# One more seven-product quad in three passes of a hybrid attention and state-space block

## The chip, the cores and the metric

The kernel runs on one core of a Trainium2 chip. The metric is device time in microseconds of one execution; before the change it is 1381.21 us, the median of three runs (1380.38 to 1382.6). Five engines work side by side, each through its own instructions in a fixed order, and wait for each other by semaphores: TensorE (PE, matrix products), VectorE (DVE), ScalarE (ACT), GpSimd (POOL) and SyncE (SP), whose queue issues nearly all DMA transfers.

## The reference

One layer on 256 rows of 2048 features, all in fp32:

```python
hn = rms_norm(x, norm_w)
q, k, v, z_a, z_s, xbc, dt_raw, g_a, g_s = split(hn @ w_in)
o_a = dilated_attention(q, k, v) * silu(z_a)            # 16 heads, three patterns
y = rms_norm(ssd_scan(conv(xbc), dt_raw) * silu(z_s))   # 4096 wide
merged = sigmoid(g_a) * (o_a @ w_attn_branch) + sigmoid(g_s) * (y @ w_ssm_branch)
out = rms_norm(x + merged @ w_out, final_norm_w)
```

Nearly all of the work is in the products with the weights: `w_in` is 2048 by some 22,600, `w_attn_branch` and `w_out` are 2048 by 2048, `w_ssm_branch` 4096 by 2048.

## The kernel before

**Precision by halves.** A weight unit is 128 x 1024 fp32 values (512 KB), fetched by SP into a ring of five buffers (tag `w`). ACT copies it into a rounded high half `h` (L279), DVE subtracts that for the low half `l` (L280), and PE makes each product from three matmuls, high by high, high by low and low by high (L485 to L487 in `triple`). The activations were split the same way.

**Passes and quads.** The second half of the kernel is mostly passes through `gemm_pair`, each making 1024 output columns of all 256 rows: the state-space branch, then v (two passes, named by their first block of 512 columns: v0, v2), the gate passes ga0 and ga2, the attention branch attn0 and attn2, and out0 and out2. Between v and ga the 16 heads' q, k and z_a are projected and the attention is done. From v on a pass sums over 16 row blocks of the weights, taken in eight quads of two: two row blocks, two halves of the rows, two blocks of 512 columns. A plain quad uses two units as they come and 24 matmuls of 512 columns. A seven-product quad is a step of Strassen's scheme in Winograd's form: seven products in place of eight, 21 matmuls. Its weights need more work. SP fetches the first unit (`wa`), half of the second (`wc`) and a combination of both made earlier (`wt`, under the name of the tile that holds it: th_a in the gate passes, fin in the attention branch). ACT and DVE split them into four pairs: ha, la from wa; hc, lc from wc; htt, ltt from wt; and, after DVE has subtracted half of wt from wa in place (L566), htu, ltu from wa (L552, L553). A number behind such a name is the unit it comes from: ga0 begins at unit 385, ga2 at 401, attn0 at 417, attn2 at 433; quad q of a pass starts at its first unit + 2q.

**Buffers that set the order.** The t and u pairs come from a pool with two buffer pairs (tags `ht`, `lt`, `bufs=2`); only the v passes have two more. The other pairs come from a pool of four. A seven-product quad adds some products directly into the outputs' accumulators (`es`, ps_ in the trace) and others into four accumulators of its own kind (`prods`, pp_), which are combined at the end of the pass by `fold` (two copies on ACT, L590 and L591, and four DVE operations, L592 to L595) and then added to the outputs (L1022 in the gate passes, L1159 in the attention branch). In the attention branch each block is then merged with the gates (L1148, L1149), and the merged rows are turned by PE transposes (`turn_m`, tiles mtp) for the output product.

**Sums made ahead.** `sum_jobs` makes the combinations wt behind certain weight units of an earlier stage, with two DVE operations each, and stores them in DRAM; those for ga, attn and out are made while the heads are projected. Likewise the activations' combinations (`sx`) are stored and fetched back by `fetch_left`: a one-element copy on GpSimd behind a named unit (L441), then a transfer on SP's queue (L442).

**What sets the order.** Each engine's order is fixed when the program is built: a scheduler walks the program with modelled times, and conversions run ahead of their use by a priority (`L_AHEAD`). The table `S_QUADS` says which quads of each pass have seven products, `G_ORDERS`, `A_ORDERS` and `V_ORDERS` in which order a pass takes its quads. PE's order interleaves a plain quad with the seven-product quads beside it.

Of the kernel before, what the change touches and what calls it, by code (L numbers as in the profile page):

```python
# [23 lines left out]
KT = D // P  # L24
UNIT = 1024
# [14 lines left out]
GS_BEFORE = {0: (0, 1), 4: (2,)}  # L40
A_ORDERS = {0: (0, 1, 2, 4, 3, 6, 5, 7), 2: (0, 2, 1, 4, 3, 5, 6, 7)}
V_ORDERS = {0: (0, 2, 4, 1, 3, 5, 6, 7), 2: (0, 2, 1, 4, 3, 5, 6, 7)}
G_ORDERS = {c: (0, 2, 1, 4, 3, 5, 6, 7) for c in (0, 2)}
O_LEFT = {0: {0: (0, 3), 4: (1, 5)}, 2: {}}
# [155 lines left out]
def hybrid_block(ctx: ExitStack, tc: tile.TileContext, wall, xt, x, pk_d, cst_d, fw_d, out):  # L200
# [34 lines left out]
    def behind_unit(n, f):  # L235
        on_unit.setdefault(n, []).append(f)
# [457 lines left out]
    with tc.tile_pool(name="ssm", bufs=2) as sp:  # L694
# [332 lines left out]
    xl = ctx.enter_context(tc.tile_pool(name="xl", bufs=1))  # L1027
    dc = xl.tile([P, 768], F32, name="dc", tag="dc")
    dist_c, count_c = dc[:, :384], dc[:, 384:]
    behind_unit(FIRST[("v", 2)] + 1, lambda behind: fetch(dc, cst_d[:, :768], behind))  # L1030
    room = room_of(big.tile([P, 6 * 512], F32, name="room_v", tag="yo0a"), 2, 2)
    with tc.tile_pool(name="vx", bufs=1) as vx:
        tl = big.tile([P, 4, UNIT], F32R, name="tl_v", tag="yo0b")
        room["tl"] = [(tl[:, 2 * n], tl[:, 2 * n + 1]) for n in range(2)]
        for n, q in enumerate(SX_V):
            fetch_left(sx_of_x, vx, len(SX_V), ("x", q), two_kts(XT, q), 0, FIRST[("v", 0)])
        for n, q in enumerate(SX_X[1:]):
            fetch_left(sx_of_x, xl, len(SX_X) - 1, ("x", q), two_kts(XT, q), 0, FIRST[("v", 0)] + 1 + n)
        for c in (0, 2):
            es, prods = gemm_pair(  # L1040
                ("v", c), lambda kt: XT[:, kt, :], KT, sx_of_x, c == 2, order=V_ORDERS[c], room=room
            )
            dst = blocks(vt, c)
            fold(prods, dst)
            for d, e in zip(dst, es):
                ve.tensor_tensor(d, e, d, ALU.add)
    sx_of_o = {}

    with tc.tile_pool(name="att", bufs=2) as ap:
# [4 lines left out]
        def scores(h, q, k, p):  # L1054
# [28 lines left out]
        def mix(h, pT, za):  # L1083
# [204 lines left out]
```

## Time and profile before

| | before |
|---|---|
| median of three runs | 1381.21 us |
| profiled execution | 1381.23 us |
| its span, first to last instruction | 1379.5 us |
| PE busy | 1368.6 us, 99% |
| DVE busy | 1169.1 us, 85% |
| ACT busy | 835.2 us, 61% |
| POOL busy | 153.5 us, 11% |
| DMA, mean | 250 GB/s |

The span is read from one profiled execution; 1.73 us of its time lie outside it. The shares are means over stages of different kinds, so the stages are read one by one, in windows and timelines. PE's matmuls are pipelined: a record is longer than the distance to the next, and the distance from start to start is what a matmul takes of the span. The same holds for rows of DVE and ACT that follow each other without a gap.

### The profile page before, as it was taken

To read this page: it belongs to the slowest core of one execution; us is meant where nothing else is said; L and a number is where in the kernel's file an instruction comes from. 1 tells how busy PE (TensorE), PEld (TensorE's weight loads), DVE (VectorE), ACT (ScalarE), POOL (GpSimd) and SP (SyncE) were. 2 spreads that over 40 slices of the span, in tenths; PEclk is the share of its full clock that TensorE was granted. 3 is DMA by queue.
4 is the path that set the end of the run, shared out by engine and by line. 5 is a ranking of instruction groups with operands and counts; after the bars stand their busy time and mean duration, and the time that the engine had idled before them with its cause. 6 is when DMAs were issued, how large, how long until landed. Compare 5 with 4: busy or idle time off the path is not lost.

```text
span 1379.5 us, 20706 instructions
## 1 busy us (share of the span) xinstructions
PE 1368.6 (99%) x7266; PEld 1167.4 (85%) x7266; DVE 1169.1 (85%) x1753; ACT 835.2 (61%) x1306; POOL 153.5 (11%) x226
## 2 busy tenths in 40 slices
PE   9999999999999999999999999999999999999997
PEld 7888888888888888888888888888888888888886
DVE  6898899888899898779989887777877788888897
ACT  7655776675667676666565554454445556655564
POOL 2301221101011100010001001211111000000122
PEclk9999999999999999999999999999999999999999
DMA  9767878778787867568677668888888757865783
GB/s 342 231 192 234 294 271 288 260 238 294 251 276 234 304 202 221 174 232 286 229 259 273 208 220 281 281 277 275 289 287 296 243 165 268 291 222 176 244 274 122
DMA packets 105080, 345.00 MB, mean 250 GB/s; under 512 B 11728, under 2 KB 13712, under 8 KB 104976
## 3 DMA queue, kind: packets, MB, share of 16 engines
q1 hardware_dynamic: 103536, 339.62, 73.7%
q10 hardware_dynamic: 1440, 4.06, 0.8%
q8 instruction: 57, 0.93, 0.3%
q14 instruction: 47, 0.39, 0.1%
HBM read 314.87 MB, written 28.77 MB: 249 GB/s over the span
## 4 chain that ended last, share of the span: by engine, by line
PE 98%; DMA 0%; DVE 0%; ACT 0%; issue 0%; SPq 0%; POOL 0%; POOLq 0%; DVEq 0%
PE ps_xs L334 8%; PE ps_zs L334 8%; PE ps_k L334 4%; PE ps_za L334 4%; PE ps_q L334 4%; PE ps_zs L340 4%; PE ps_xs L340 4%; PE ps_ssm L486 3%; PE ps_ssm L487 3%; PE ps_ssm L485 3%; PE ps_q L340 2%; PE ps_za L340 2%; PE ps_k L340 2%; PE ps_gs L423 2%; PE ps_gs L422 2%; PE ps_gs L421 2%
## 5 line engine op out<-in xcount | busy, mean ns | idle before, releaser
L279 ACT ACTIVATE h<-w 128x1024 fp32r<-128x1024 f32 (+1 forms) x398 | 413.5, 1048 | 308.2 <-issue 80.2
L280 DVE TENSOR_TENSOR l<-w,h 128x1024 fp32r<-128x1024 f32 (+1 forms) x398 | 478.5, 1209 | 116.5 <-ACT h L279 112.1
L334 PE MATMUL ps_zs<-XT,h 128*128 128x512 f32 x496 | 172.0, 393 | 0.0
L334 PE MATMUL ps_xs<-XT,h 128*128 128x512 f32 x496 | 171.6, 394 | 0.0
L340 PE MATMUL ps_zs<-XT,l 128*128 128x256 f32 x496 | 134.6, 279 | 0.0
L340 PE MATMUL ps_xs<-XT,l 128*128 128x256 f32 x496 | 133.7, 278 | 0.0
L334 PEld LDWEIGHTS ps_xs<-XT,h 128*128 128x128 f32 x496 | 91.4, 188 | 19.4
L334 PEld LDWEIGHTS ps_zs<-XT,h 128*128 128x128 f32 x496 | 91.3, 188 | 18.9
L340 PEld LDWEIGHTS ps_zs<-XT,l 128*128 128x128 f32 x496 | 93.4, 188 | 2.1
L340 PEld LDWEIGHTS ps_xs<-XT,l 128*128 128x128 f32 x496 | 93.2, 188 | 2.1
L334 PE MATMUL ps_q<-XT,h 128*128 128x512 f32 x256 | 91.1, 404 | 0.0
L334 PE MATMUL ps_k<-XT,h 128*128 128x512 f32 x256 | 88.6, 395 | 0.0
L334 PE MATMUL ps_za<-XT,h 128*128 128x512 f32 x256 | 88.4, 394 | 0.0
L552 ACT ACTIVATE ha<-wa 128x1024 fp32r<-128x1024 f32 x43 | 45.4, 1055 | 44.7 <-PE ps_ssm L487 10.2
L340 PE MATMUL ps_q<-XT,l 128*128 128x256 f32 x256 | 68.5, 278 | 0.0
L340 PE MATMUL ps_k<-XT,l 128*128 128x256 f32 x256 | 68.4, 278 | 0.0
L340 PE MATMUL ps_za<-XT,l 128*128 128x256 f32 x256 | 68.4, 277 | 0.0
L553 DVE TENSOR_TENSOR la<-wa,ha 128x1024 fp32r<-128x1024 f32 x43 | 52.4, 1218 | 10.1 <-ACT ha L552 9.3
L553 DVE TENSOR_TENSOR ltu<-wa,htu 128x1024 fp32r<-128x1024 f32 x38 | 46.3, 1219 | 15.3 <-ACT htu L552 15.2
L795 ACT ACTIVATE gt<-acb,acT 128x128 f32<-128x128 f32 x128 | 44.1, 390 | 23.7 <-DMA acb<-acum_d 23.7
L334 PEld LDWEIGHTS ps_k<-XT,h 128*128 128x128 f32 x256 | 47.0, 188 | 9.8
L334 PEld LDWEIGHTS ps_q<-XT,h 128*128 128x128 f32 x256 | 47.1, 188 | 9.6
(688 smaller groups left out, 3328.0 us busy)
## 6 DMA issues: line engine op xcount, KB each, us to landing
w<-in_wall SPq DMA_DIRECT2D x394, 512.0 KB, 4.8
wa<-in_wall SPq DMA_DIRECT2D x43, 512.0 KB, 4.8
th_a<-in_wall SPq DMA_DIRECT2D x19, 512.0 KB, 5.5
sums_at<-in_wall SPq DMA_DIRECT2D x18, 512.0 KB, 5.0
acb<-acum_d SPq DMA_DIRECT2D x32, 256.0 KB, 3.7
t_ssm<-sums_at SPq DMA_DIRECT2D x13, 512.0 KB, 4.6
wt<-t_ssm SPq DMA_DIRECT2D x13, 512.0 KB, 4.9
th_a<-in_wall SPq DMA_DIRECT2D x19, 256.0 KB, 5.9
```

The lines of the kernel that those rows point to most:

```text
L279: ac.activation(h[:, a:b], w[:, a:b], AF.Copy)
L280: ve.tensor_tensor(l[:, a:b], w[:, a:b], h[:, a:b].bitcast(F32), ALU.subtract)
L334: high = pe.matmul(acc, h[:, kk, :], xs_of(kt), start=(kt == 0), stop=False)
L340: low = pe.matmul(acc[:, S:], l[:, kk, :], xs_of(kt)[:, :S], start=False, stop=(kt == KT - 1))
L421: pe.matmul(accs[i], xh, h[:, kk], start=(kt == 0), stop=False)
L422: pe.matmul(accs[i], xh, l[:, kk], start=False, stop=False)
L485: pe.matmul(acc, xh, h, start=start, stop=False)
L486: pe.matmul(acc, xh, l, start=False, stop=False)
L487: pe.matmul(acc, xl, h, start=False, stop=stop)
L552: ac.activation(h, src, AF.Copy)
L553: ve.tensor_tensor(l, src, h.bitcast(F32), ALU.subtract)
L795: ac.activation(g4[:, n, b], acb[:, j, b // 2 * P : b // 2 * P + P], AF.Relu, scale=-1.0, bias=sc[:, h : h + 1],)
```

## The change

In both gate passes quad 3 becomes a seven-product quad, and the quads are taken in the order 0, 2, 4, 1, 3, 5, 6, 7, as in v0: the plain quad 1 parts 2 and 4 from the run 3, 5, 6. In attn0 quad 5 becomes one, and the order is 0, 1, 2, 4, 5, 6, 3, 7: two plain quads, four seven-product quads, two plain ones. Three more sums are made ahead (22 for 19), one every 3.75 units from the fourth unit of the heads on, where it was every fourth from the eighth. The activations' combination of quad 3, which had a pool of its own in the v passes, joins the others in the pool that lasts through the gate passes. The tile `dc` with the heads' distances and counts goes: these are now fetched into the mask's place and two other pieces, by three small transfers. Three small tiles of `rsqrt_rows` become one. The fetches of the activations' combinations for the attention branch (sx_o) go from SP's queue to GpSimd's, and the first of them is tied to unit 404 where it was 408. The lines behind L40 move up by one to five: L279 becomes L278, L552 L551, L592 L591, L1148 L1143, L1159 L1154.

```diff
-A_ORDERS = {0: (0, 1, 2, 4, 3, 6, 5, 7), 2: (0, 2, 1, 4, 3, 5, 6, 7)}
+A_ORDERS = {0: (0, 1, 2, 4, 5, 6, 3, 7), 2: (0, 2, 1, 4, 3, 5, 6, 7)}
 V_ORDERS = {0: (0, 2, 4, 1, 3, 5, 6, 7), 2: (0, 2, 1, 4, 3, 5, 6, 7)}
-G_ORDERS = {c: (0, 2, 1, 4, 3, 5, 6, 7) for c in (0, 2)}
+G_ORDERS = {c: (0, 2, 4, 1, 3, 5, 6, 7) for c in (0, 2)}
...
-    ("v", 0): (2, 3, 4, 5, 6), ("v", 2): (2, 4, 5, 6), ("ga", 0): (2, 4, 5, 6), ("ga", 2): (2, 4, 5, 6),
-    ("attn", 0): (2, 4, 6), ("attn", 2): (2, 4, 5, 6), ("out", 0): (3, 5), ("out", 2): (3, 5),
+    ("v", 0): (2, 3, 4, 5, 6), ("v", 2): (2, 4, 5, 6), ("ga", 0): (2, 3, 4, 5, 6), ("ga", 2): (2, 3, 4, 5, 6),
+    ("attn", 0): (2, 4, 5, 6), ("attn", 2): (2, 4, 5, 6), ("out", 0): (3, 5), ("out", 2): (3, 5),
 }
...
-SX_X = (2, 4, 5, 6)
-SX_V = (3,)
-O_BEHIND = 7, 14, 15, 17
+SX_X = (2, 4, 3, 5, 6)
+O_BEHIND = 3, 14, 15, 17
...
-LEFT_EVERY, ATT_EVERY = 11, 4
+LEFT_EVERY = 11
...
-    def fetch_left(kept, pool, bufs, key, x, spare, u):
+    def fetch_left(kept, pool, bufs, key, x, spare, u, queue=nc.sync):
         def get(behind):
             sx = new_sx(pool, bufs, spare, f"{key[0]}{key[1]}")
             gp.tensor_copy(sx[:, 0, 0, 0:1], behind)
-            nc.sync.dma_start(sx.bitcast(F32), lefts[key])
+            queue.dma_start(sx.bitcast(F32), lefts[key])
             kept[key[1]] = left_parts(sx, x, spare)
...
     def rsqrt_rows(sums, n, name):
-        var = lead.tile([P, 2], F32, name=f"var_{name}", tag="var", bufs=1)
+        rows = lead.tile([P, 3, 2], F32, name=f"rows_{name}", tag="rows", bufs=1)
+        var, r, hr = rows[:, 0], rows[:, 1], rows[:, 2]
...
-        for n, q in enumerate(SX_X + SX_V):
+        for n, q in enumerate(SX_X):
             behind_unit(begin + 3 + n * LEFT_EVERY, lambda behind, q=q: left_x(q, behind))
...
-    dc = xl.tile([P, 768], F32, name="dc", tag="dc")
-    dist_c, count_c = dc[:, :384], dc[:, 384:]
-    behind_unit(FIRST[("v", 2)] + 1, lambda behind: fetch(dc, cst_d[:, :768], behind))
+    count = lead.tile([P, P], F32, name="count", tag="cw"), cst[:, 512:768]
+    for n, (dst, a) in enumerate(((mask3, 0), (count[0], 384), (count[1], 512))):
+        behind_unit(FIRST[("v", 2)] + n, lambda behind, dst=dst, a=a: fetch(dst, cst_d[:, a : a + dst.shape[-1]], behind))
     room = room_of(big.tile([P, 6 * 512], F32, name="room_v", tag="yo0a"), 2, 2)
-    with tc.tile_pool(name="vx", bufs=1) as vx:
-        tl = big.tile([P, 4, UNIT], F32R, name="tl_v", tag="yo0b")
-        room["tl"] = [(tl[:, 2 * n], tl[:, 2 * n + 1]) for n in range(2)]
-        for n, q in enumerate(SX_V):
-            fetch_left(sx_of_x, vx, len(SX_V), ("x", q), two_kts(XT, q), 0, FIRST[("v", 0)])
-        for n, q in enumerate(SX_X[1:]):
-            fetch_left(sx_of_x, xl, len(SX_X) - 1, ("x", q), two_kts(XT, q), 0, FIRST[("v", 0)] + 1 + n)
+    tl = big.tile([P, 4, UNIT], F32R, name="tl_v", tag="yo0b")
+    room["tl"] = [(tl[:, 2 * n], tl[:, 2 * n + 1]) for n in range(2)]
+    for n, q in enumerate(SX_X[1:]):
+        fetch_left(sx_of_x, xl, len(SX_X) - 1, ("x", q), two_kts(XT, q), 0, FIRST[("v", 0)] + n)
...
         sum_jobs(
-            SUMS_ATT, range(FIRST[("q", 0)] + 7, N_UNITS, ATT_EVERY),
+            SUMS_ATT, [FIRST[("q", 0)] + 3 + n * 15 // 4 for n in range(len(SUMS_ATT))],
...
         for n, q in enumerate(ATT_QUADS):
             fetch_left(
-                sx_of_o, xl if n else xk, max(1, n and len(SX_X) - 1), ("o", q), two_kts(oaT, q), 0, FIRST[("ga", 2)] + O_BEHIND[n]
+                sx_of_o, xl if n else xk, max(1, n and len(SX_X) - 1), ("o", q), two_kts(oaT, q), 0, FIRST[("ga", 2)] + O_BEHIND[n], nc.gpsimd
             )
```

DVE's order at the end of attn0, before. The names are those of the pairs above; the last number of each is a serial number of the tile. ltu429 is the last pair of attn0's last seven-product quad, l427 to l432 are its last plain quads' low halves, 433 and later belong to attn2:

```order
L553 TENSOR_TENSOR ltu429_12492<-wa429_12474,htu429_12491 128x1024
L280 TENSOR_TENSOR l427_12519<-w427_12516,h427_12518 128x1024
L280 TENSOR_TENSOR l428_12525<-w428_12522,h428_12524 128x1024
L592 TENSOR_TENSOR fin_12270<-pp_attn0_2_12352,fin_12270 128x512
L280 TENSOR_TENSOR l431_12555<-w431_12552,h431_12554 128x1024
L280 TENSOR_TENSOR l432_12561<-w432_12558,h432_12560 128x1024
L593 TENSOR_TENSOR fin_12270<-pp_attn0_3_12353,fin_12270 128x512
L553 TENSOR_TENSOR ltt437_12693<-fin_12270,htt437_12692 128x1024
L594 TENSOR_TENSOR fin_12270<-fin_12270 128x512
L280 TENSOR_TENSOR l433_12642<-w433_12639,h433_12641 128x1024
```

and now:

```order
L552 TENSOR_TENSOR ltu427_12493<-wa427_12475,htu427_12492 128x1024
L552 TENSOR_TENSOR ltt429_12531<-fin_12307,htt429_12530 128x1024
L279 TENSOR_TENSOR l432_12604<-w432_12601,h432_12603 128x1024
L552 TENSOR_TENSOR ltu429_12535<-wa429_12517,htu429_12534 128x1024
L591 TENSOR_TENSOR fin_12307<-pp_attn0_2_12389,fin_12307 128x512
L552 TENSOR_TENSOR ltt437_12736<-fin_12307,htt437_12735 128x1024
L1154 TENSOR_TENSOR fin_12307<-ps_attn0_0_12308,fin_12307 128x512
L592 TENSOR_TENSOR fin_12307<-pp_attn0_3_12390,fin_12307 128x512
L1143 SCALAR_TENSOR_TENSOR th_a_7802<-th_a_7802,fin_12307 128x512
L593 TENSOR_TENSOR fin_12307<-fin_12307 128x512
L279 TENSOR_TENSOR l433_12685<-w433_12682,h433_12684 128x1024
L1144 SCALAR_TENSOR_TENSOR th_s_90<-th_a_7802,th_s_90 128x512
```

The plain quads' l431 and l432 stood behind ltu429 and the first step of the fold; now they stand ahead of it, and the whole fold, the additions and the merge stand behind it, between the conversions of attn2.

DVE's order at the opening of attn2, a little further on, before:

```order
L553 TENSOR_TENSOR la437_12684<-wa437_12679,ha437_12683 128x1024
L1148 SCALAR_TENSOR_TENSOR th_a_7806<-th_a_7806,fin_12270 128x512
L1149 SCALAR_TENSOR_TENSOR th_s_90<-th_a_7806,th_s_90 128x512
L566 TENSOR_TENSOR wa437_12679<-wa437_12679,fin_12270 128x1024
L1149 SCALAR_TENSOR_TENSOR th_s_90<-th_a_7806,th_s_90 128x512
L553 TENSOR_TENSOR lc437_12688<-fin_12270,hc437_12687 128x512
L280 TENSOR_TENSOR l435_12724<-w435_12721,h435_12723 128x1024
L280 TENSOR_TENSOR l436_12730<-w436_12727,h436_12729 128x1024
L553 TENSOR_TENSOR ltu437_12697<-wa437_12679,htu437_12696 128x1024
```

and now (the row of l434 stands two ahead of the first one):

```order
L552 TENSOR_TENSOR lc437_12731<-fin_12307,hc437_12730 128x512
L1154 TENSOR_TENSOR fin_12307<-ps_attn0_2_12310,fin_12307 128x512
L1154 TENSOR_TENSOR fin_12307<-ps_attn0_3_12311,fin_12307 128x512
L1143 SCALAR_TENSOR_TENSOR th_a_7802<-th_a_7802,fin_12307 128x512
L279 TENSOR_TENSOR l435_12767<-w435_12764,h435_12766 128x1024
L565 TENSOR_TENSOR wa437_12722<-wa437_12722,fin_12307 128x1024
L1143 SCALAR_TENSOR_TENSOR th_a_7802<-th_a_7802,fin_12307 128x512 x2
L279 TENSOR_TENSOR l436_12773<-w436_12770,h436_12772 128x1024
L1144 SCALAR_TENSOR_TENSOR th_s_90<-th_a_7802,th_s_90 128x512
L552 TENSOR_TENSOR la441_12805<-wa441_12800,ha441_12804 128x1024
L1144 SCALAR_TENSOR_TENSOR th_s_90<-th_a_7802,th_s_90 128x512
L552 TENSOR_TENSOR ltu437_12740<-wa437_12722,htu437_12739 128x1024
```

Before, all twelve additions and merge steps stood between l434 and l435, and between l435 and ltu437 only l436. Now three stand between l434 and l435, and between l435 and ltu437 stand the subtraction into wa437, four merge steps, l436 and la441.

ACT's order in ga0, before, from the pair a of unit 395 (quad 5) on:

```order
L552 ACTIVATE ha395_11788<-wa395_11783 128x1024
L552 ACTIVATE hc395_11792<-wc395_11785 128x512
L552 ACTIVATE htt395_11797<-th_a_7806 128x1024
L552 ACTIVATE htu395_11801<-wa395_11783 128x1024
L552 ACTIVATE ha397_11831<-wa397_11826 128x1024
L552 ACTIVATE hc397_11835<-wc397_11828 128x512
L279 ACTIVATE h399_11871<-w399_11869 128x1024
L279 ACTIVATE h400_11877<-w400_11875 128x1024
```

and now:

```order
L551 ACTIVATE ha395_11818<-wa395_11813 128x1024
L551 ACTIVATE hc395_11822<-wc395_11815 128x512
L551 ACTIVATE htu391_11788<-wa391_11770 128x1024
L551 ACTIVATE ha397_11861<-wa397_11856 128x1024
L551 ACTIVATE hc397_11865<-wc397_11858 128x512
L551 ACTIVATE htt395_11827<-th_a_7802 128x1024
L278 ACTIVATE h399_11901<-w399_11899 128x1024
L278 ACTIVATE h400_11907<-w400_11905 128x1024
L551 ACTIVATE htu395_11831<-wa395_11813 128x1024
```

htu395 stood ahead of ha397 and of the plain units 399 and 400; now it stands behind all of them, and the quad of unit 391, which was plain, has its htu391 among the others.

## Rows read from the trace of the kernel before

**Rows 1.** The page: busy us (share) of the engines, PE's clock by slices.
```profile
PE 1368.6 (99%) x7266; PEld 1167.4 (85%) x7266; DVE 1169.1 (85%) x1753; ACT 835.2 (61%) x1306; POOL 153.5 (11%) x226
...
PEclk9999999999999999999999999999999999999999
```

**Rows 2.** The page: the chain that ended last, by engine.
```profile
PE 98%; DMA 0%; DVE 0%; ACT 0%; issue 0%; SPq 0%; POOL 0%; POOLq 0%; DVEq 0%
```

**Rows 3.** PE's waits: us in total, times, the longest.
```profile
PE warm L632 <- DVE ssq L629: 1.4, 1, 1.4
PE ps_first L386 <- ACT h L279: 1.2, 1, 1.2
```

**Rows 4.** Busy us (instructions) by stretches, then clock, DMA share, GB/s.
```profile
800.00:1100.00 300.00, 300.00 (x1717) 262.44 (x1716) 230.04 (x418) 151.06 (x226) 44.84 (x57) 1.00 0.81 273
1100.00:1150.00 50.00, 50.00 (x250) 42.27 (x249) 39.57 (x67) 28.47 (x40) 0.00 (x0) 1.00 0.56 181
1150.00:1200.00 50.00, 50.00 (x223) 41.44 (x223) 44.06 (x47) 31.39 (x38) 3.16 (x4) 1.00 0.82 289
1200.00:1250.00 50.00, 50.00 (x227) 41.38 (x226) 44.30 (x51) 27.80 (x33) 0.00 (x0) 1.00 0.65 216
```

**Rows 5.** Timeline of PE, attn0 to attn2: start, length, instruction, count.
```profile
1212.83 0.39 PE L485 MATMUL ps_attn<-hc,sx_o 128*128 128x512 f32 x1
...
1225.53 0.39 PE L487 MATMUL ps_attn<-htu,oaTb 128*128 128x512 f32 x1
...
1243.21 0.39 PE L487 MATMUL ps_attn<-h,oaTa 128*128 128x512 f32 x1
...
1248.66 0.82 PE L1141 MATMUL mtp<-cst,th_s 128*128 128x128 f32 x6
1249.23 0.48 PE L485 MATMUL ps_attn<-hc,sx_o 128*128 128x512 f32 x1
...
1251.61 0.39 PE L486 MATMUL ps_attn<-l,oaTa 128*128 128x512 f32 x1
```

**Rows 6.** Timeline of DVE, end of ga2 to the opening of attn2.
```profile
1197.39 0.69 DVE L592 TENSOR_TENSOR th_a<-pp_ga,th_a 128x512 f32<-128x512 f32 x1 [1.64 <-PE pp_ga L487]
...
1207.67 1.21 DVE L566 TENSOR_TENSOR wa<-wa,fin 128x1024 f32<-128x1024 f32 x1
...
1227.05 1.23 DVE L553 TENSOR_TENSOR ltu<-wa,htu 128x1024 fp32r<-128x1024 f32 x1 [1.50 <-ACT htu L552]
...
1230.46 0.68 DVE L592 TENSOR_TENSOR fin<-pp_attn,fin 128x512 f32<-128x512 f32 x1
...
1243.87 0.68 DVE L1148 SCALAR_TENSOR_TENSOR th_a<-th_a,fin 128x512 f32<-128x512 f32 x1
1244.47 1.21 DVE L553 TENSOR_TENSOR la<-wa,ha 128x1024 fp32r<-128x1024 f32 x1
...
1249.15 2.35 DVE L280 TENSOR_TENSOR l<-w,h 128x1024 fp32r<-128x1024 f32 x2
```

**Rows 7.** Timeline of ACT in attn0, idle time before it in brackets.
```profile
1225.95 1.06 ACT L552 ACTIVATE htu<-wa 128x1024 fp32r<-128x1024 f32 x1 [0.31 <-PE ps_attn L487]
1226.92 3.89 ACT L279 ACTIVATE h<-w 128x1024 fp32r<-128x1024 f32 x4
```

**Rows 8.** DMA issues, 1100 to 1340: count, KB, median us to landing.
```profile
w<-in_wall SPq DMA_DIRECT2D x53, 512.0 KB, 4.6
...
th_a<-t_ga SPq DMA_DIRECT2D x6, 512.0 KB, 4.2
...
sx_o<-sxd_o SPq DMA_DIRECT2D x4, 512.0 KB, 5.6
```

**Rows 9.** Timeline of POOL: two of the four copies ahead of sx_o.
```profile
1176.81 1.24 POOL L441 CAST sx_o<-h 128x1 fp32r<-128x1 f32 x1 [109.18 <-ACT h L279]
...
1198.17 0.18 POOL L441 CAST sx_o<-h 128x1 fp32r<-128x1 f32 x1 [7.43 <-PE pp_ga L487]
```

**Rows 10.** Timeline of SP's queue: the last issue of sx_o.
```profile
1198.38 0.33 SPq L442 DMA_DIRECT2D sx_o<-sxd_o  x1
```

More of the change, by code (lines that the diff above doesn't have):

```diff
@@ L602, in rsqrt_rows @@
     def rsqrt_rows(sums, n, name):
-        var = lead.tile([P, 2], F32, name=f"var_{name}", tag="var", bufs=1)
+        rows = lead.tile([P, 3, 2], F32, name=f"rows_{name}", tag="rows", bufs=1)
+        var, r, hr = rows[:, 0], rows[:, 1], rows[:, 2]
         ve.tensor_scalar(var, sums, 1.0 / n, EPS, ALU.mult, ALU.add)
-        r = lead.tile([P, 2], F32, name=f"r_{name}", tag="rr", bufs=1)
         gp.tensor_tensor(r, var, half, ALU.pow)
-        hr = lead.tile([P, 2], F32, name=f"hr_{name}", tag="hr", bufs=1)
         ve.tensor_scalar(hr, r, 0.5, None, ALU.mult)
@@ L1027, in hybrid_block @@
     xl = ctx.enter_context(tc.tile_pool(name="xl", bufs=1))
-    dc = xl.tile([P, 768], F32, name="dc", tag="dc")
-    dist_c, count_c = dc[:, :384], dc[:, 384:]
-    behind_unit(FIRST[("v", 2)] + 1, lambda behind: fetch(dc, cst_d[:, :768], behind))
+    count = lead.tile([P, P], F32, name="count", tag="cw"), cst[:, 512:768]
+    for n, (dst, a) in enumerate(((mask3, 0), (count[0], 384), (count[1], 512))):
+        behind_unit(FIRST[("v", 2)] + n, lambda behind, dst=dst, a=a: fetch(dst, cst_d[:, a : a + dst.shape[-1]], behind))
     room = room_of(big.tile([P, 6 * 512], F32, name="room_v", tag="yo0a"), 2, 2)
-    with tc.tile_pool(name="vx", bufs=1) as vx:
-        tl = big.tile([P, 4, UNIT], F32R, name="tl_v", tag="yo0b")
-        room["tl"] = [(tl[:, 2 * n], tl[:, 2 * n + 1]) for n in range(2)]
-        for n, q in enumerate(SX_V):
-            fetch_left(sx_of_x, vx, len(SX_V), ("x", q), two_kts(XT, q), 0, FIRST[("v", 0)])
-        for n, q in enumerate(SX_X[1:]):
-            fetch_left(sx_of_x, xl, len(SX_X) - 1, ("x", q), two_kts(XT, q), 0, FIRST[("v", 0)] + 1 + n)
[L1039 to L1046, printed above, removed]
+    tl = big.tile([P, 4, UNIT], F32R, name="tl_v", tag="yo0b")
+    room["tl"] = [(tl[:, 2 * n], tl[:, 2 * n + 1]) for n in range(2)]
+    for n, q in enumerate(SX_X[1:]):
+        fetch_left(sx_of_x, xl, len(SX_X) - 1, ("x", q), two_kts(XT, q), 0, FIRST[("v", 0)] + n)
+    for c in (0, 2):
+        es, prods = gemm_pair(
+            ("v", c), lambda kt: XT[:, kt, :], KT, sx_of_x, c == 2, order=V_ORDERS[c], room=room
+        )
+        dst = blocks(vt, c)
+        fold(prods, dst)
+        for d, e in zip(dst, es):
+            ve.tensor_tensor(d, e, d, ALU.add)
     sx_of_o = {}
@@ L1059, in scores @@
             slope = 2.0 ** (-8.0 * (h + 1) / NH)
-            ve.scalar_tensor_tensor(t, dist_c, slope / SCALE, sps[:, :384], ALU.mult, ALU.add)
+            ve.scalar_tensor_tensor(t, mask3, slope / SCALE, sps[:, :384], ALU.mult, ALU.add)
             st = ap.tile([P, 8], F32, name=f"st{h}", tag="st", bufs=1)
@@ L1069, in scores @@
                 ve.scalar_tensor_tensor(
-                    p[:, a:b], p[:, a:b], 1.0, count_c[:, a:b], ALU.mult, ALU.mult,
+                    p[:, a:b], p[:, a:b], 1.0, count[i], ALU.mult, ALU.mult,
                     accum_out=st[:, 4 + i : 5 + i],
```

## The prediction, made before the changed kernel had run

> **What bounds the kernel now.** I read the page's busy shares first, then the chain that ended last, then what TensorE (PE) waited for, and last the timelines of the stages that the change touches. PE is busy for 99% of the span, its granted clock at nine tenths or more in every slice [rows 1]; the chain is 98% PE [rows 2]; and in the whole run PE waits for other work only twice, 1.4 and 1.2 us, both before the first projections [rows 3]. So the span is the PE instruction stream laid end to end. Time can be won only by issuing fewer matmuls, and lost wherever PE has to wait. What remains to be read is how much room stands behind PE where the change adds work: in the gate passes and the attention branch's first pass DVE is busy 39.6 to 44.3 us of 50, ACT 28 to 31, and the DMA engines 0.56 to 0.82 of the time, the clock 1.00 throughout [rows 4]. DVE has least to give.
>
> **What is removed.** Three plain quads of 24 matmuls become seven-product quads of 21: nine 512-column matmuls fewer, and nothing else leaves PE. From the start of the row at 1225.53 to that at 1243.21 us PE issues 78 of them without a gap [rows 5]: 17.68 / 78 = 0.227 us each. 9 x 0.227 = 2.04 us, 0.148% of the time. That is all there is to gain.
>
> **What is added at the opening of the attention branch's second pass.** A seven-product quad makes four operand pairs (a, c, t, u), the last behind a subtraction into wa. Its t and u pairs come from a pool of two buffer pairs, so a new u pair can be made only when PE has finished the one before the last. Before, the last seven-product quad of the first pass stood well ahead of its end: its ltu was made at 1227.05 and the folding of the seven products began at 1230.46 [rows 6], while PE first needed the l of unit 435, in the second pass, at 1251.61 [rows 5]. DVE ended that l, the first of two in 2.35 us from 1249.15, at about 1250.4 [rows 6], 1.2 us ahead. Now the plain quads 3 and 7 come last in the order, PE interleaves them with quads 5 and 6, and the last u pair is made late: DVE's new order has ltu429 ahead of the whole of the fold, the merge and the conversions that open the second pass.
>
> The durations, from rows: two 128x1024 subtractions take 2.35 us and the record of one is 1.22, so one takes 1.13 from start to start; a 128x512 one 0.60 (1243.87 to 1244.47) [rows 6]. ACT's 128x1024 copy has a record of 1.06 us and takes 0.97 in a row (four in 3.89) [rows 7]. ACT started htu at 1225.95, 0.03 us after the end of PE's matmul of 1225.53 + 0.39, the last on its buffer [rows 5, 7], and DVE started ltu 0.04 us after ACT's end (1225.95 + 1.06 to 1227.05) [rows 6, 7].
>
> Count from the start of PE's last matmul on htu427, whose end frees the buffer. To the start of ltu429 it is 0.39 + 0.03 + 1.06 + 0.04 = 1.52 us. From there DVE has, one after another, five 1024-wide operations (ltu429, ltt437, l433, l434, la437), twelve 512-wide ones (four of the fold, four additions of the other sums, three of the merge, lc437), then l435 to its end, 1.22, and 0.03 to PE: 1.52 + 5 x 1.13 + 12 x 0.60 + 1.25 = 15.62. PE has 65 matmuls and 2 transposes before it needs l435: 65 x 0.227 + 2 x 0.10 (six transposes from 1248.66 to 1249.23 [rows 5]) = 14.96. PE waits 0.66 us. The next need is l436: DVE has the subtraction into wa437, two merge steps and l436, 1.13 + 1.20 + 1.13 = 3.46, against ten matmuls, 2.27: 1.19 more. Then ltu437: 0.60 + 1.13 + 0.60 + 1.13 = 3.46 against nine matmuls and eight transposes, 2.84: 0.62 more. Together 2.47 us. No transfer stands in this chain, so it does not hang on the traffic; 1% on DVE's durations moves it by 0.2. If ltu429 started 2.5 us sooner than counted all of it would vanish; 1 us later, and it would be 3.5. I take 2.47.
>
> **What is added in the gate passes.** Three seven-product quads now follow each other, with two buffer pairs and a five-deep ring for fetched weights. In ACT's order htu395 stood ahead of the conversions of w399 and w400; now it stands behind both. The fetch of w400 waits for a ring buffer until DVE has made ltu391. Counted from PE's last matmul on htt393: 0.39 + 0.03 + 1.06 + 0.04 + 1.22 = 2.74 to the end of ltt391; la395, lc395, the subtraction into wa395 and ltu391, 3 x 1.13 + 0.60 = 3.99; the landing; then h400 and htu395 on ACT, 2.03, and 0.10 for issue and handoffs: 8.86 + landing. PE needs htu395 58 matmuls on, after 13.17 us. So it waits for the landing minus 4.3. A 512 KB weight landed in 4.6 us here at the median, a gate pass's sum in 4.2, the slowest such fetch's median was 5.6 [rows 8]: 0.3 at 4.6, nothing at 4.2, 1.3 at 5.6. Two more places are built alike (htu389 in the first pass, ha407 in the second). Three times 0.3 is 0.9; a wait in one gives room to the next, so I take 0.7, between 0 and 3.9.
>
> **What hides.** Three more sums are made during the heads' projections: each two 512-wide DVE operations, two fetches and a store. That is 3.6 us in a stretch where DVE is busy 230 of 300 us, and 3.75 MB beside the 82 MB that 273 GB/s give, at 0.81 of the DMA engines [rows 4]. PE's order there is unchanged and PE never waits; I cost it at nothing, and at most 3.6 us if DVE's room failed. The shared small tiles, the reloaded mask (three small fetches for one) and the v pass's fetches, one buffer pool for two, sit under the same cover: nothing, at most 0.5 us if the first head's scores waited for the mask; none gives a gain, since PE does not wait for any of them now.
>
> The four fetches of sx_o go from SP's queue to GpSimd's. The last was issued at 1198.38 [rows 10] and PE's first use of any of them is at 1212.83 [rows 5]; less the 5.6 us of landing [rows 8] even this pairing leaves 8.8 us. The 1-element copy that goes ahead of each on GpSimd took 0.18 us once and 1.24 another time [rows 9], as if it had stood behind one DVE subtraction of 1.22. The Trainium skill, "SBUF — State Buffer", section "SBUF: two separate sides", says that a DMA issued from GpSimd has its descriptors written by that engine, that certain DVE operations hold a port pair which the two share, and that a transfer of some 620 ns can then take 3100. The copies agree with it; no run here shows it for a transfer yet, and by it alone a fetch would land some 2.5 us later.
>
> **The sum.** The profiled run took 1381.23 us (the span of 1379.5 and 1.73 around it); the median of the runs shown is 1381.21, so nothing is shifted. 1381.23 - 2.04 + 2.47 + 0.70 = 1382.36: a loss of 0.08%.
>
> **Rivals.**
> 1. The gain is kept whole: 1381.23 - 2.04 = 1379.2. For it: every wait above is the difference of two long sums, and PE waits nowhere in these stages today [rows 3]. Against it: the second pass's opening had only 1.2 us of room with the fold 20 us ahead of it [rows 5, 6], and what now fills DVE there is counted without any transfer. With the gate passes free and only this wait as counted the time is 1381.7, which still belongs to the forecast.
> 2. Slower: the ring in the gate passes. It decides where weights land in over 5.1 us at all three places: 3 x 0.8 = 2.4 us, and with -2.04 + 2.47 the loss passes 0.2%. At 5.6 it is 3.9 us and the time 1385.6. For it: the second gate pass moves 289 GB/s with the DMA engines at 0.82 [rows 4], and each new quad fetches 1.25 MB for 1.0. Against it: the medians of 4.6 and 4.2 [rows 8] and the 0.56 of the 50 us before.
> 3. GpSimd's fetches late. It decides where one is held for more than 8.8 us. DVE works from 1197.39 to 1208.9 with hardly a gap [rows 6]; held for all of these 11.5 us a fetch would cost 2.7: 1385.1. This is the rule of the page named above carried from one operation to a train; the copies were held for one.
>
> **How the numbers follow.** What a measurement of this kernel tells from no change is 0.2%, 2.76 us: faster is below 1378.45, slower above 1383.97. The forecast's case, 1380.5 to 1383.9, has 0.66; rival 1 0.13; rival 2 0.16; rival 3 0.02; and 0.03 goes to a gain beyond the removed matmuls, which no row explains. The whole gain is itself under 0.2%, so rival 1 counts as the same: faster 0.03, same 0.79, slower 0.18. The range runs from rival 1's time to the beginning of rival 2: 1379.2 to 1384.4.
>
> **What would show it.** In the profile after: PE waits for low halves (l and ltu) in the second attention pass, about 0.7, 1.2 and 0.6 us within 7 us; DVE without a gap from ltu429 to ltu437; up to three waits of some tenths for htu or ha in the gate passes, following their landings; no wait in the projections. It is wrong if PE shows no wait at the opening of the second pass (rival 1), if the gate passes hold over 2.3 us of waits (rival 2), or if sx_o is waited for (rival 3).

## The result, and the profile after

The changed kernel takes 1382.89 us (median of 22 runs, 1381.89 to 1385.51), the kernel before 1380.85 in 22 runs made beside them: a ratio of 1.0016, with a 95% interval of 1.001 to 1.0022. It is 2.0 us slower: a loss clear of its interval, though smaller than the 0.2% that the prediction took as the least difference a measurement can tell. The prediction had 1382.4 and a loss of 1.1 us in a range from 1379.2 to 1384.4.

The profiled execution took 1382.62 us, its span is 1380.8. The page's engine row, which answers to [rows 1]:

```profile
PE 1368.6 (99%) x7257; PEld 1165.0 (84%) x7257; DVE 1182.4 (86%) x1768; ACT 841.8 (61%) x1312; POOL 156.0 (11%) x241
```

Nine PE instructions fewer, as counted, and 13 us more of DVE; the granted clock is nine tenths or more in every slice, as before. The waits of PE, which answer to [rows 3] (us in total, times, the longest):

```profile
PE warm L630 <- DVE ssq L627: 1.4, 1, 1.4
PE ps_attn L485 <- DVE l L279: 1.2, 2, 0.7
PE ps_first L385 <- ACT h L278: 0.8, 1, 0.8
PE ps_out L484 <- ACT fin L589: 0.7, 1, 0.7
PE ps_attn L485 <- DVE ltu L552: 0.2, 1, 0.2
```

Three kinds are new, all between 1248 and 1284 us: the low halves and ltu of attn2, and a wait of the output product's first pass for ACT's copy in the fold. Stretch by stretch, as in [rows 4]:

```profile
1100.00:1150.00 50.00, 49.98 (x248) 41.88 (x247) 42.37 (x69) 29.77 (x42) 0.00 (x0) 1.00 0.57 185
1150.00:1200.00 50.00, 49.98 (x222) 41.04 (x221) 46.43 (x49) 33.37 (x40) 9.62 (x8) 1.00 0.84 286
1200.00:1250.00 50.00, 49.51 (x220) 40.53 (x219) 44.76 (x50) 30.81 (x36) 0.00 (x0) 1.00 0.66 224
1250.00:1300.00 50.00, 48.29 (x218) 38.88 (x217) 46.74 (x59) 26.45 (x32) 4.01 (x2) 1.00 0.64 209
```

DVE has 2.4 to 2.8 us more in the gate passes; PE's loss, as far as whole records show it, lies after 1200 us.

**The opening of attn2.** DVE's timeline from the last u pair of attn0 on, which answers to [rows 6] (start, length, instruction; idle time before it in brackets):

```profile
1234.57 1.23 DVE L552 TENSOR_TENSOR ltu<-wa,htu 128x1024 fp32r<-128x1024 f32 x1 [3.29 <-ACT htu L551]
1235.71 0.68 DVE L591 TENSOR_TENSOR fin<-pp_attn,fin 128x512 f32<-128x512 f32 x1
...
1247.45 1.22 DVE L279 TENSOR_TENSOR l<-w,h 128x1024 fp32r<-128x1024 f32 x1
...
1250.93 1.21 DVE L279 TENSOR_TENSOR l<-w,h 128x1024 fp32r<-128x1024 f32 x1
...
1254.40 1.21 DVE L552 TENSOR_TENSOR ltu<-wa,htu 128x1024 fp32r<-128x1024 f32 x1
```

ACT's, at the copy htu429 which that ltu429 waits for:

```profile
1233.47 1.06 ACT L551 ACTIVATE htu<-wa 128x1024 fp32r<-128x1024 f32 x1 [3.46 <-PE ps_attn L486]
```

and PE's at the two low halves and at ltu, which answers to [rows 5]:

```profile
1233.05 0.39 PE L486 MATMUL ps_attn<-htu,oaTb 128*128 128x512 f32 x1
...
1247.84 0.39 PE L484 MATMUL ps_attn<-h,oaTa 128*128 128x512 f32 x1
1248.72 0.50 PE L485 MATMUL ps_attn<-l,oaTa 128*128 128x512 f32 x1 [0.49 <-DVE l L279]
1249.06 0.40 PE L486 MATMUL ps_attn<-h,oaTa 128*128 128x512 f32 x1
...
1252.20 0.50 PE L485 MATMUL ps_attn<-l,oaTa 128*128 128x512 f32 x1 [0.74 <-DVE l L279]
...
1255.67 0.50 PE L485 MATMUL ps_attn<-ltu,oaTa 128*128 128x512 f32 x1 [0.24 <-DVE ltu L552]
```

The last matmul on htu427 started at 1233.05 and ended at 1233.44; ACT, idle for 3.46 us, began htu429 0.03 us behind it, and ltu429 started at 1234.57, 1.52 us after the start of the count as worked out. l435 ended at 1247.45 + 1.22 = 1248.67, 15.62 us after that start; the prediction has 15.59 there (its 15.62 holds 0.03 more, to PE). A wait is read as the distance to the next start less the 0.227 of one matmul: 1248.72 - 1247.84 - 0.23 = 0.65 us for l435; 1.02 for l436, found in the same way; 0.46 for ltu437. After each wait the next matmul comes 0.34 us later and not 0.227, which adds 0.11 each time. Together 0.65 + 1.02 + 0.46 + 3 x 0.11 = 2.46 us, where 2.47 was predicted. That the totals agree to 0.01 us is partly luck: the prediction counts no restart. The first two restarts only fill time in which PE would have waited for the next low half, but the last, 0.11, comes on top, and the wait without it is 2.35.

**The opening of out0.** This wait was not predicted. Timelines of ACT, of GpSimd and of PE there:

```profile
1283.09 0.35 ACTq L646 DMA_DIRECT2D fin<-in_x  x1
1283.49 0.60 ACT L589 ACTIVATE fin<-pp_attn 128x512 f32<-128x512 f32 x1 [2.97 <-POOL fin L645]
```
```profile
1279.44 3.62 POOL L645 COPY fin<-h 128x1 f32<-128x1 f32 x1 [82.49 <-ACT h L278]
```
```profile
1283.03 0.39 PE L486 MATMUL pp_attn<-htt,sx_o 128*128 128x512 f32 x1
1284.14 0.50 PE L484 MATMUL ps_out<-h,mT 128*128 128x512 f32 x1 [0.72 <-ACT fin L589]
```

At 1283.09 ACT issues the fetch of x into fin. The issue stands in ACT's queue behind a one-element copy that GpSimd makes to time it, and this copy lasted 3.62 us. Behind the issue stands the fold's copy out of an accumulator (pp_attn), and for this copy PE waits with the first matmul of out0: 1284.14 - 1283.03 - 0.23 = 0.88 us, and about 0.1 for the restart. In the kernel before the same copy lasted 3.16 us and ACT stood before the same issue, but the first copy of the fold had already been made at 1276.08:

```profile
1279.60 3.16 POOL L647 COPY fin<-h 128x1 f32<-128x1 f32 x1 [81.25 <-ACT h L279]
```
```profile
1276.08 0.60 ACT L590 ACTIVATE fin<-pp_attn 128x512 f32<-128x512 f32 x1 [1.23 <-PE pp_attn L487]
...
1283.19 0.53 ACT L287 ACTIVATE sx_m<-spare 128x384 fp32r<-128x384 f32 x1 [3.65 <-POOL fin L647]
```

**The gate passes.** Two short waits remain in the profile after, 0.19 and 0.18 us with a restart of 0.11 each, at 1149.36 (htu395, the predicted place) and at 1168.75 (the first high half of a plain unit in ga2): 0.59 us. So -2.04 + 2.46 + 0.99 + 0.59 = 2.00, close to the 2.04 between the medians. (The two profiled executions, from which the waits are read, differ by less, 1382.62 - 1381.23 = 1.39: the one after began ga0's matmuls 0.43 us earlier, at 1116.59 for 1117.02, and from there to the end it is 1.8 us longer, so 0.2 us of the sum are not located.) The transfers of the stretch 1100 to 1340, for [rows 8]:

```profile
w<-in_wall SPq DMA_DIRECT2D x46, 512.0 KB, 4.7
...
sx_o<-sxd_o POOLq DMA_DIRECT2D x4, 512.0 KB, 7.8
```

### The profile page after: what moved, and what is told of

Read it like the earlier page. It is cut to its first block, busy times and chain, and to the rows that moved or that the text cites. A ratio compares the mean times of both kernels' runs of the same rounds, so it can differ in the third digit from the quotient of the medians.

```text
span 1380.8 us, 20758 instructions
## 1 busy us (share of the span) xinstructions
PE 1368.6 (99%) x7257; PEld 1165.0 (84%) x7257; DVE 1182.4 (86%) x1768; ACT 841.8 (61%) x1312; POOL 156.0 (11%) x241
## 4 chain that ended last, share of the span: by engine, by line
PE 95%; issue 2%; DVE 2%; DMA 0%; POOL 0%; ACT 0%; SPq 0%; POOLq 0%; ACTq 0%; DVEq 0%
PE ps_xs L333 8%; PE ps_zs L333 8%; PE ps_za L333 4%; PE ps_k L333 4%; PE ps_q L333 4%; PE ps_zs L339 4%; PE ps_xs L339 4%; PE ps_ssm L485 3%; PE ps_ssm L486 3%; PE ps_ssm L484 3%; PE ps_q L339 2%; PE ps_k L339 2%; PE ps_za L339 2%; PE ps_gs L421 2%; PE ps_gs L422 2%; PE ps_gs L420 2%
## 5 line engine op out<-in xcount | busy, mean ns | idle before, releaser
L278 ACT ACTIVATE h<-w 128x1024 fp32r<-128x1024 f32 (+1 forms) x392 | 408.1, 1048 | 310.9 <-issue 62.4
L279 DVE TENSOR_TENSOR l<-w,h 128x1024 fp32r<-128x1024 f32 (+1 forms) x392 | 471.9, 1209 | 108.3 <-ACT h L278 103.6
L551 ACT ACTIVATE ha<-wa 128x1024 fp32r<-128x1024 f32 x46 | 48.6, 1057 | 46.0 <-DMA wa<-in_wall 10.3
L552 DVE TENSOR_TENSOR la<-wa,ha 128x1024 fp32r<-128x1024 f32 x46 | 56.1, 1219 | 9.0 <-ACT ha L551 8.8
L552 DVE TENSOR_TENSOR ltu<-wa,htu 128x1024 fp32r<-128x1024 f32 x41 | 49.9, 1218 | 14.9 <-ACT htu L551 14.7
L551 ACT ACTIVATE htu<-wa 128x1024 fp32r<-128x1024 f32 x41 | 43.2, 1054 | 22.1 <-PE ps_ssm L486 7.2
```

The source lines that it names most:

```text
L278: ac.activation(h[:, a:b], w[:, a:b], AF.Copy)
L279: ve.tensor_tensor(l[:, a:b], w[:, a:b], h[:, a:b].bitcast(F32), ALU.subtract)
L551: ac.activation(h, src, AF.Copy)
L552: ve.tensor_tensor(l, src, h.bitcast(F32), ALU.subtract)
```

## The experiments

The time of each is compared with runs of the kernel before on the same chip. The theories: A, the loss is made in the attention branch, by DVE's train and by ACT's late copy; B, it is made in the gate passes, by the ring and its landings; C or F, the wait at out0 comes from the place of the fetch in a queue and from the copy on GpSimd; D, the fold is late by itself.

### e1: the gate passes alone

```diff
-    ("attn", 0): (2, 4, 5, 6), ...
+    ("attn", 0): (2, 4, 6), ...
-A_ORDERS = {0: (0, 1, 2, 4, 5, 6, 3, 7), ...
+A_ORDERS = {0: (0, 1, 2, 4, 3, 6, 5, 7), ...
```

> The changed kernel with attn0 put back (three seven-product quads, its old order); both gate passes keep their five. Theory A (the loss is made in the attention branch: DVE's train at the opening of attn2, and ACT's fold copy late at the opening of out0): six matmuls fewer, -1.36 us, and 0.2 to 0.5 of short waits in the gate passes, so about 1 us under before, with no PE wait at attn2's l and none for ACT's fold at out0. Theory B (the loss is made in the gate passes by the ring and the landings): +0.5 us or more over before, with waits of over 1 us for htu or ha there.

1380.70 us against 1380.91, ratio 0.9999 (0.999 to 1.0008). PE's waits after the opening are one:

```profile
PE pp_ga L484 <- ACT htu L551: 0.5, 1, 0.5
```

The time alone does not decide: 0.2 us under before lies between A's 1 us under and B's 0.5 over, and the interval holds both. The waits do: without the fourth quad in attn0 both waits of the attention branch are gone, as theory A has it. But the gain that A expected is not there. From the first matmul of ga0 to the first transpose of attn2 the trace has 130.08 us, where before it had 130.27: 0.19 less, not 1.36. The gate passes took back nearly 1.2. ACT's and DVE's timelines show the chain that was written down for htu395:

```profile
1147.27 1.06 ACT L278 ACTIVATE h<-w 128x1024 fp32r<-128x1024 f32 x1 [1.88 <-DMA w<-in_wall]
1148.23 1.04 ACT L551 ACTIVATE htu<-wa 128x1024 fp32r<-128x1024 f32 x1
```
```profile
1141.05 1.22 DVE L552 TENSOR_TENSOR ltu<-wa,htu 128x1024 fp32r<-128x1024 f32 x1
```

ltu391 ends at 1142.27, h400 waits on ACT for its landing until 1147.27, htu395 stands behind it and ends at 1149.27 and PE, which was there 0.67 us earlier, starts at 1149.33. The mechanism of the prediction is right there, and its 0.7 us stand between the 0.59 of the profile after and the 1.1 here. The size goes with the landing: in the eight profiles with five seven-product quads in ga0 the fetch of w400 landed 4.24 to 4.87 us after its issue, and PE waited 0.04 to 0.67 us for htu395, each time the landing less 4.2. The prediction had the landing less 4.3.

### e2: attn0 alone

```diff
-    ("ga", 0): (2, 3, 4, 5, 6), ("ga", 2): (2, 3, 4, 5, 6),
+    ("ga", 0): (2, 4, 5, 6), ("ga", 2): (2, 4, 5, 6),
-G_ORDERS = {c: (0, 2, 4, 1, 3, 5, 6, 7) for c in (0, 2)}
+G_ORDERS = {c: (0, 2, 1, 4, 3, 5, 6, 7) for c in (0, 2)}
```

> The changed kernel with both gate passes put back (four seven-product quads, old order); attn0 keeps four in its new order. Theory A: three matmuls fewer, -0.68, and the waits of the attention branch, 2.1 to 2.5 at the opening of attn2 and 0.9 at the opening of out0: about +2.5 us over before, more than the whole change. Theory B: -0.7 to 0 against before.

1384.55 us, ratio 1.0033 (1.0022 to 1.0045): 3.6 us over before, more than the whole change, as theory A has it, and more than the 2.5 expected. The waits:

```profile
PE ps_attn L485 <- DVE l L279: 1.0, 2, 0.6
PE ps_out L484 <- ACT fin L589: 0.7, 1, 0.7
PE ps_attn L485 <- DVE ltu L552: 0.3, 1, 0.3
PE ps_attn L485 <- DVE la L552: 0.2, 1, 0.2
```

By the list four waits stand in attn2's opening, and a fifth gap of 0.4 us, where the whole change has three; the one at out0 is the same. From the first matmul of ga0 to the end this profile has 3.3 us more than before's with three matmuls fewer, so PE lost 4.0 us there, 1.0 at out0 and 3.0 at attn2, where the whole change lost 2.46. Why attn2 loses 0.5 us more behind the old gate passes is not shown.

### e3 and e6: the wait at out0

e3 issues the fetches of x from SP's queue; e6 leaves them on ACT's and lets ACT make the one-element copy.

```diff
-    ... fetch(fin[:, i, cs], x[i * P : (i + 1) * P, cs], behind, nc.scalar),
+    ... fetch(fin[:, i, cs], x[i * P : (i + 1) * P, cs], behind),          # e3
+    ... fetch_a(fin[:, i, cs], x[i * P : (i + 1) * P, cs], behind),        # e6
+    def fetch_a(dst, src, behind):                                         # e6
+        ac.activation(dst[:, 0:1], behind, AF.Copy)
+        nc.scalar.dma_start(dst, src)
```

> The changed kernel with the fetches of x into fin (behind units of out0 and out2) issued by SP's queue and not by ACT's. In the profile after, ACT stands 3 us behind such an issue, which waits for a one-element copy on GpSimd, and the fold's copy stands behind it, for which PE waits 0.9 us. Theory C (the place in ACT's queue makes that wait): the wait of ps_out goes, 0.9 us less than the changed kernel, the waits of attn2 stay as they are. Rival D (the fold is late by itself, since the pass before ended late on DVE and ACT): the wait stays, or moves to the next thing within 0.3 us, and the time stays.

> The changed kernel with only that: the copies ahead of the fetches of x are made by ACT. Theory F: ACT does not stand before its fold copy, the wait of ps_out (0.88 us) goes, attn2's three waits stay (2.46 with their restarts): about 1.1 to 1.3 us over before, as e3. Rival D (the fold is late by itself): the wait stays, 2.0 over before.

e3 took 1382.30 us, ratio 1.0010 (1.0002 to 1.0019); e6 1382.17, ratio 1.0011 (1.0002 to 1.0020). In both the wait of ps_out is gone and those of attn2 stand as they were. e6's:

```profile
PE ps_attn L485 <- DVE l L279: 1.2, 2, 0.7
...
PE ps_attn L485 <- DVE ltu L552: 0.2, 1, 0.2
```

So the wait came not from a fold late by itself (D), but from its place behind an issue that GpSimd held (C, F). The times stand 1.4 and 1.65 us over before, where the changed kernel has 2.0; 0.9 less was expected. The intervals are wider than these differences, and the verdict rests on the waits.

### e4, e8 and e5: the fourth quad with more buffer pairs

e4 gives attn0 two more (ht, lt) pairs, in the region of XT, which nothing reads after ga2; it puts the plain quad 3 between the seven-product quads, and the fetches of x on SP's queue as e3. e5 is e4 with e6's copies. e8 is e5 without the buffer pairs.

```diff
-A_ORDERS = {0: (0, 1, 2, 4, 5, 6, 3, 7), ...
+A_ORDERS = {0: (0, 1, 2, 4, 3, 6, 5, 7), ...
+        tl_a = big.tile([P, 4, UNIT], F32R, name="tl_a", tag="xm")
         attend(0)
...
-                ("attn", c), ..., order=A_ORDERS[c], room=room
+                ("attn", c), ..., order=A_ORDERS[c], room=room if c else
+                {**room, "tl": [(tl_a[:, 2 * n], tl_a[:, 2 * n + 1]) for n in range(2)]}
```

> The changed kernel with two more (ht, lt) buffer pairs in attn0, in the place of the activations that are dead by then, attn0's four seven-product quads in the order 0, 1, 2, 4, 3, 6, 5, 7 (a plain quad between the second and the third of them), and the fetches of x on SP's queue. Theory A (the last u pair is made late because it waits for a buffer, and the fold and merge pile up behind it): the last ltu comes earlier, the waits at attn2 fall from 2.1 to under 0.5 us, and with 0.9 less at out0 the time is 1.0 to 1.7 us under before. Rival E (DVE has too much work in the branch whatever the order): waits of about 2 us stay in attn0 or attn2, and the time stays within 0.5 us of e3.

e4 took 1385.96 us, ratio 1.0039 (1.0026 to 1.0051): neither theory's time. But the waits of the attention branch are down to 0.2 us, as A has it; one of another kind has come, at out0:

```profile
PE pp_out L484 <- ACT htt L551: 3.4, 1, 3.4
```

The timelines of GpSimd, of SP's queue and of ACT show how:

```profile
1290.38 8.21 POOL L645 COPY fin<-h 128x1 f32<-128x1 f32 x1 [8.81 <-ACT h L278]
```
```profile
1288.63 0.33 SPq L530 DMA_DIRECT2D wa<-in_wall  x1
1298.62 0.33 SPq L646 DMA_DIRECT2D fin<-in_x  x1
```
```profile
1310.79 1.06 ACT L551 ACTIVATE htt<-room_o 128x1024 fp32r<-128x1024 f32 x1 [8.04 <-DMA room_o<-t_out]
```

The copy ahead of the second fetch of x began at 1290.38 and lasted 8.21 us. DVE worked all that time, in ten operations on operands in SBUF. SP's queue stood from 1288.6 to 1298.6 behind the fetch which that copy gates; out0's combination (room_o) was fetched late, ACT stood 8.0 us for its landing, and PE 3.6.

> As e4 (four (ht, lt) pairs in attn0, its order 0, 1, 2, 4, 3, 6, 5, 7), but the fetches of x stay on ACT's queue and the one-element copy ahead of each is made by ACT, not by GpSimd. In e4 PE waited 0.2 us in the attention branch and 3.6 at the opening of out0, where SP's queue stood for 10 us behind a GpSimd copy of 8.2 us. Theory F (the copy waits as long as DVE works on two operands in SBUF without a pause, and holds the queue it gates): no copy is held, the fetches of out0 issue in time, the 3.6 us go, and with 0.6 to 1.1 of gate waits the time is 1.0 to 1.4 us under before. Rival G (out0's combination lands late because the two buffer pairs took a region, or because the traffic is denser): a wait for htt of over 1 us stays in out0.

e5 took 1380.37 us against 1380.52, ratio 0.9997 (0.9988 to 1.0006). By the list PE's waits are those of the start alone:

```profile
PE warm L630 <- DVE ssq L627: 1.4, 1, 1.4
PE ps_first L385 <- ACT h L278: 0.4, 1, 0.4
```

> As e5 without the two more buffer pairs: attn0's order 0, 1, 2, 4, 3, 6, 5, 7 and the copies by ACT. Theory A (the buffer pairs set how late the last u pair is): about 2 us of waits stay at the opening of attn2 although the order is e5's. Rival H (it was the order that took the waits away in e4): under 0.5 us of waits.

e8, one run, took 1384.71 us; its waits:

```profile
PE ps_attn L485 <- DVE l L279: 1.7, 1, 1.7
...
PE ps_attn L484 <- ACT h L278: 0.3, 1, 0.3
```

The last ltu of attn0 in DVE's timeline, first of e5, then of e8, whose gate passes began 0.75 us later:

```profile
1230.50 1.22 DVE L552 TENSOR_TENSOR ltu<-wa,htu 128x1024 fp32r<-128x1024 f32 x1
```
```profile
1235.11 1.21 DVE L552 TENSOR_TENSOR ltu<-wa,htu 128x1024 fp32r<-128x1024 f32 x1
```

In e8 ACT began that pair's htu 0.08 us after the end of PE's last matmul on the u pair before. With the order of e5 and two pairs the last u pair is made 3.9 us later and PE stands for 1.9 us from start to start (1.71 in the list); with four pairs it is not so. Two buffer pairs make the last u pair late, as theory A says. One run gives no interval for e8's time, so this rests on the rows. F holds too: with ACT's copies nothing of e4's 3.6 us is left.

### e9 and e10: what of it pays

e9 is e5 with ga0 put back, e10 is e5 with both gate passes put back, by the edit of e2.

> As e5, but the first gate pass (ga0) put back to four seven-product quads in its old order: attn0 with four buffer pairs, ga2 with five. The gate waits seen so far: 0.2 to 0.7 with restarts of 0.1 at ga0's htu395, where ACT stands before a landing, and 0.3 to 0.7 in ga2. Six matmuls fewer, -1.36, 0.3 in attn0 and attn2, 0.3 to 0.6 in ga2: 0.5 to 0.8 under before, with no wait at 1149 us. If e5's time stays at before's although its profile shows 1.6 us less after the opening of ga0, and this one's falls below it, ga0's wait on the landing is what spreads e5's runs; if both stay at before's time, the rest is in what varies from run to run.

> As e5 with both gate passes put back: only attn0 has its fourth seven-product quad, with four buffer pairs, the order 0, 1, 2, 4, 3, 6, 5, 7 and the copies by ACT. Three matmuls fewer, -0.68, and 0.3 at the opening of attn2: 0.4 under before. Against e2 (the same quad with two pairs, the order of the change and GpSimd's copies), 4.1 us less: the cost of the fourth quad was in its buffers and queue, not in the quad.

e9: 1380.09 against 1380.55, ratio 0.9998 (0.9989 to 1.0007). e10: 1380.74 against 1380.55, ratio 1.0001 (0.9992 to 1.0010). e10 is 0.2 us over before where e2 is 3.6: where its buffers and queue are provided for, the fourth quad costs nothing that can be measured. But neither shows a gain. e1, e5, e9 and e10 remove 3 to 9 matmuls, 0.7 to 2.0 us, and all lie within 0.5 us of before, their intervals reaching 0.1% to either side. No version was found that beats the kernel before by more than can be measured. From the first matmul of ga0 to the end the profiles of e5, e9 and e10 are shorter than before's, by 1.6, 1.0 and 0.8 us (260.8, 261.4 and 261.6 for 262.4). What stands ahead of ga0 varies by as much: all twelve profiles have the same 6119 PE instructions there, in the same order, and up to the 1201st of them, the first 222 us, which the gate passes and attn0 have no part in, they take 221.0 to 222.8 us (222.0 in before's, 222.8 in e10's). So in a single run a gain of this size drowns in what varies at its start. e5's profile is also of the fastest of its 11 runs (1379.45), and why their median gains only 0.15 us is not settled; a gain of 1.6 would lie at the edge of its interval.

### e7: the fetches of sx_o on SP's queue

```diff
-                ... FIRST[("ga", 2)] + O_BEHIND[n], nc.gpsimd
+                ... FIRST[("ga", 2)] + O_BEHIND[n]
```

> The changed kernel with the four fetches of sx_o back on SP's queue. In the profile after they landed 7.8 us after their issue by GpSimd, 5.6 before. The prediction: their room hides it, so the landing goes back to about 5.6 and the time stays (within 0.5 us of the changed kernel). Rival 3 of the prediction: sx_o late costs something that the wait list does not show, and the time falls by over 0.5 us.

Both expectations were wrong. e7 took 1389.52 us, ratio 1.0068 (1.0055 to 1.0082): 9.0 us over before, where the changed kernel has 2.0. The landing went back, to a median of 4.0 us, but the copies on GpSimd now gate SP's queue, with the weights behind; each of the four issues stands 0.02 or 0.03 us behind the end of its copy. Two new waits:

```profile
PE ps_attn L484 <- ACT h L278: 0.5, 1, 0.5
...
PE pp_ga L484 <- ACT htt L551: 0.2, 1, 0.2
```

The profile is of the shortest run (1384.78) and shows a part: waits for a high half at the opening of attn0 and for htt in ga2, 0.7 us by the list, beside those known. The other four runs took 1389.38 to 1391.69, and no profile shows where; a copy may have been held longer in them, which is not shown.

## Why the prediction was right, and what it left out

**What is removed**: right. Nine matmuls, 2.04 us. Rival 1, the whole gain kept, is out with the waits at attn2.

**attn2's opening**: right to 0.1 us, in place, in the three waits (0.66, 1.19 and 0.62 predicted; 0.76, 1.13 and 0.57 with their restarts) and in the cause. e5 and e8 show the cause apart from the trace: with two more buffer pairs DVE's train starts earlier and the waits go, at the same order without them PE waits again. It could be counted so closely because no transfer stands in it.

**The gate passes**: right in size, 0.7 for 0.59 in the profile after and 1.1 in e1, and in the rule for htu395, the landing less 4.3 us. That the total came so near is partly luck, since half of the 0.59 stands at a place that was not foreseen (0.18 us and a restart). Of the three places named htu395 was there each time, ha407 only in e3 (0.44 us) and e6 (0.16), htu389 never.

**What hides**: right for the projections and the small tiles, where PE shows no new wait: from the 1201st PE instruction to the first of ga0 the profiles before and after both take 895.03 us. For sx_o the result was right, no wait, and a premise wrong: that a copy on GpSimd is held for one DVE operation. A copy ahead of sx_o lasted 4.19 us after and 6.65 in e5, with no wait of PE behind either, and the copies ahead of x 3.62 and 8.21 (e4). The Trainium skill, "SBUF — State Buffer", section "SBUF: two separate sides", says that the port pair which DVE and GpSimd share is held for a whole instruction. The runs agree where a copy of 1.24 us ends with one DVE operation [rows 9], and show more: a copy can stand behind a whole train, as behind the ten operations in the 8.21 us, and the copies of 3.16, 3.62, 4.19 and 8.21 us all ended within 0.05 us of a pause in DVE's work (in e4 one of 0.04 us). Not every copy waits for a pause: before the change one of 1.24 us, from 1188.37, ended with the first of two DVE subtractions that follow each other. What decides is open. With the transfers on GpSimd's queue a landing took 7.8 us, where SP's took 5.6 [rows 8] and 4.0 (e7). That is 2.2 us later than before, near the 2.5 that the prediction drew from the 3100 ns of that section of the Trainium skill; but the figure there is for a transfer beside a DVE tensor_copy, DVE ran tensor_tensor here, and no run shows whether DVE's work made the difference.

**The step that is missing**: nothing in the sum stood for the opening of out0, 0.99 us, half of the measured loss and as much as the difference between 1.1 predicted and 2.0 found. The change moves the fold's first copy in ACT's order from ahead of the fetch of x to behind it. The rows for it were in the trace of before: GpSimd's copy of 3.16 us and ACT's idle time of 3.65 behind it, shown above. They were passed over because nobody who mattered waited for them then. Rival 2 (the ring) did not decide; at 0.59 us its waits are far from 2.4. Rival 3 named the mechanism at the wrong place: it looked at the transfers that GpSimd issues, not at the queues that wait for its copies.

## What to carry to other kernels

Where an engine is busy for 99%, count what an edit takes from it, and then walk the order of each other engine from the instruction that comes late to the first thing the busy engine needs from it: the sum of start-to-start times was right here to 0.1 us. In that walk, count the DMA issues of a compute engine's queue as instructions that can wait: whatever moves behind one waits for its gate. And do not let GpSimd time a transfer while VectorE has a long train on SBUF; a one-element copy by ScalarE took 0.18 to 0.20 us (e5, e6) and cost PE nothing.

## What the runs showed of the hardware

A wait of PE has a second price. After waits of up to 1.0 us from start to start the next matmul came 0.34 us later instead of 0.227, and all was as before. After the 1.9 us of e8 the granted clock fell; windows of e8 (columns as in [rows 4]) and the rows of PE behind the wait:

```profile
1252.00:1256.00 4.00, 4.00 (x13) 3.12 (x13) 4.00 (x6) 0.00 (x0) 0.00 (x0) 0.64 0.91 261
1256.00:1262.00 6.00, 5.69 (x33) 4.63 (x32) 4.33 (x6) 2.51 (x5) 0.00 (x0) 1.00 0.37 139
```
```profile
1251.24 0.66 PE L485 MATMUL ps_attn<-l,oaTa 128*128 128x512 f32 x1 [1.71 <-DVE l L279]
1251.70 0.63 PE L486 MATMUL ps_attn<-h,oaTa 128*128 128x512 f32 x1
...
1255.00 0.40 PE L485 MATMUL ps_attn<-l,oaTa 128*128 128x512 f32 x1
```

The nine matmuls from 1251.24 to 1255.00 took 3.76 us, mostly 0.43 each, nearly twice 0.227: the lower of the two levels, 1.2 GHz. At the higher level 9 x 0.227 = 2.04 would have done. Then they came at 0.23 again. The clock fell also behind the wait of 3.6 us in e4 (0.66 in the 4 us from 1313 on). So the gap of 1.9 us in e8 cost another 1.7, and one of 1.0 in the changed kernel another 0.1.
